# Fewer second keys in the first gate pass, and the fetched rows behind it, in a retention, convolution and expert-retrieval step

## The chip, the cores and the metric

The kernel runs on one core of a Trainium2 chip. The core has five engines that run side by side, each with its own queue taken in order: TensorE (PE; its weight loads are listed as PEld), VectorE (DVE), ScalarE (ACT), GpSimd (POOL) and SyncE (SP), which here only starts transfers. Sixteen DMA engines move data between the memory and the on-chip buffers. The metric is the device time of one execution in microseconds, lower is better.

## The reference

The step is one decoder layer for a prompt of 512 tokens and for 32 sampled tokens (8 sequences of 4): an input projection, retention and a convolution module side by side, an output projection and a layer norm. Behind these comes the part that the change touches, a retrieval of experts by product keys:

```python
q = (xb @ w_query).reshape(PEER_BLOCK, PEER_HEADS, PEER_DQ)     # 8 heads
s1 = jnp.einsum('phd,hkd->phk', q1, sub_keys_1)                  # 128 first keys
s2 = jnp.einsum('phd,hkd->phk', q2, sub_keys_2)                  # 128 second keys
v1, i1 = lax.top_k(s1, PEER_TOPK)                                # 16 of each
v2, i2 = lax.top_k(s2, PEER_TOPK)
...                                                              # the best 16 of the pairs
idx = e1 * N_KEYS + e2                                           # one of 16384 experts
gate = jax.nn.softmax(sv)
u = jnp.take(peer_u, idx, axis=0)
act = jax.nn.gelu(jnp.einsum('phkd,pd->phk', u, xb))
vv = jnp.take(peer_v, idx, axis=0)
out = jnp.einsum('phk,phkd->pd', gate * act, vv)
```

So each token takes 8 x 16 = 128 experts. Each is a row of 1024 numbers in the first table (u) and one in the second (v). The output is the gated sum of second-table rows, and a second layer norm ends the layer.

## The kernel before

The retrieval is done in two ways at once.

**Fetched rows.** For the first 288 tokens (two groups of 128 prompt tokens and the 32 sampled ones) the rows are fetched. One indirect transfer (L564, GpSimd's queue) brings the u and the v row of one expert for each of 128 partitions, 1 MB. VectorE takes the dot with the token (L567), ScalarE the gelu and the gate (L569, L570), and VectorE adds the weighted v row to a running sum (L575). The first group of 128 tokens has 128 such rows and is done ahead of the stages that matter here. Then come the sampled group "s" (32 tokens, spread over four times as many partitions, 32 rows) and the second prompt group "b" (128 rows), 160 rows in all. The transfers share three buffers (pool `gp`), and a buffer is free when its v row has been added.

**Whole tables.** For the last 256 prompt tokens (`ND`) both tables are read whole, one second key at a time: a key `e` covers 128 experts, so a tile of each table is 512 KB, and SyncE loads it into one of five buffers (pool `uvp`, `UV = 5`).

- `scores_of(e)` (L774) multiplies the u tile with the 256 tokens, and ScalarE applies the gelu.
- `build` makes the gates. For eight tokens at a time (`TB`) VectorE writes a one-hot table over the first keys (`A`, L847), one over the second keys (`M`, L849), and `B`, which is `M` times the gate in three bf16 parts (L852). TensorE multiplies `A` with `B`, three products a token (L858), so that a token's gates lie as 128 first keys by `ne` second keys in PSUM. The tables have two buffers each, and so has the PSUM tile.
- `v_stage(e)` (L893) multiplies key `e`'s gated scores, from a tile `GW`, with the v tile, and adds into four PSUM banks (`pB`), eight matmul records a key.

All 128 keys' gated scores for 256 tokens don't fit at once, so the keys lie in four tiles, `EG = (32, 20, 44, 32)` from `E0S = (0, 32, 52, 96)`: Gb, Gc, Ga and Gd. The scores of Ga and Gb (76 keys) are made first. `first_keys` builds the gates of keys 0 to 95 and multiplies them into Gb and Ga (L872); into Gc, whose scores don't exist yet, it copies them (L870). `last_keys` builds those of 96 to 127 once Gb's keys have been used and its room is free, and ScalarE copies them into Gd (L878). For Gc and Gd `s_stage(e)` makes the scores late and VectorE multiplies them in (L885).

`run((phases(), 1), (fetched(), 2))` interleaves the two ways in program order, one key's step to two rows. The program order isn't the order on the chip: a scheduler orders each engine's queue ahead of time, from its own estimate of when each instruction can start. `behind(a, b)` adds an order between two instructions for that scheduler. On the chip each engine then takes its queue strictly as written.

`finish` ends a fetched group: residual, layer norm, and an output transfer in SyncE's queue (L585), among the table loads. The last layer norm (L445 to L453) reads the four PSUM banks, and L945 stores its result.

Of the kernel before, what the change touches and what calls it, by code (L numbers as in the profile page):

```python
# [8 lines left out]
F32 = mybir.dt.float32  # L9
# [4 lines left out]
AF = mybir.ActivationFunctionType  # L14
OP = mybir.AluOpType
# [3 lines left out]
D = 1024  # L19
# [5 lines left out]
PH, NK, TK = 8, 128, 16  # L25
# [5 lines left out]
ND = NR - NG2  # L31
TB = 8
KX = 60
UV = 5
EG = (32, 20, 44, 32)
E0S = (0, 32, 52, 96)

ROWS = [(a, TK // (a + 1)) for a in range(TK)]
NCAND = sum(n for _, n in ROWS)
# [52 lines left out]
def tile_step(ctx: ExitStack, tc: tile.TileContext, a, o):  # L92
    nc = tc.nc
    V, S, T, G = nc.vector, nc.scalar, nc.tensor, nc.gpsimd
# [68 lines left out]
    def behind(ins, other):  # L163
        tc.add_manual_dep(ins.ins, other.ins.name, mybir.DependencyInfo(
            mybir.DependencyClass.NoSync, mybir.DependencyReason.DATA), reason="order")
# [342 lines left out]
    def retrieve(q_of, hs, w, r, E, gate, e0, later=None):  # L508
# [47 lines left out]
        V.reciprocal(sm[:n], sm[:n])  # L556
        V.tensor_mul(gate[:n, e0:e0 + nh], ex[:n], sm[:n].unsqueeze(2).to_broadcast([n, nh, TK]))

    def gather(x1, idx, gate, acc, slots):

        for k in slots:
            t = (gx.tile([128, 2 * D], F32, name="g") if x1 is x1_0 and k < KX and k % 4 == 3 else
                 gp.tile([128, 2 * D], F32, name="g"))
            G.indirect_dma_start(out=t, out_offset=None, in_=a["uv"],  # L564
                                 in_offset=bass.IndirectOffsetOnAxis(ap=idx[:, k:k + 1], axis=0))
            act = gw.tile([128, 2], F32, name="act")
            V.scalar_tensor_tensor(t[:, :D], t[:, :D], 1.0, x1, op0=OP.mult, op1=OP.mult, accum_out=act[:, 0:1])  # L567
            wgt = gw.tile([128, 1], F32, name="wgt")
            S.activation(act[:, 1:2], act[:, 0:1], AF.Gelu)  # L569
            S.activation(wgt, act[:, 1:2], AF.Copy, scale=gate[:, k:k + 1])  # L570
            v = t[:, D:]
            if k == slots[0]:
                S.activation(acc, v, AF.Copy, scale=wgt)
            else:
                V.scalar_tensor_tensor(acc, v, wgt, acc, op0=OP.mult, op1=OP.add)  # L575
            yield
# [72 lines left out]
    pm, last = mix_mm(128, g0, y0, 0, wo)  # L649
# [100 lines left out]
    gap = ctx.enter_context(tc.tile_pool(name="gap", bufs=1, reuse_waits="tile"))  # L750
# [7 lines left out]
    banks[:] = [pq]  # L758
    load_keys()
    ln2 = [bc_row("lng", a["ln2_g"], D), bc_row("lnb", a["ln2_b"], D)]  # L760
    GW = {2: gap.tile([128, EG[2], ND], F32, name="Ga")}

    def place(e):

# [30 lines left out]
    for g in range(2):  # L795
# [9 lines left out]
        p = mmps().rearrange("p (q t) -> p q t", q=4)  # L805
# [10 lines left out]
                V.tensor_sub(gr, gr, gtT[:, q, cs])  # L816
    topk_of("b", NS, range(0, PH, 2))
    topk_of("s", 0, range(2))
    for e in range(E0S[2], E0S[3]):
        S.activation(place(e), scores_of(e), AF.Gelu)  # L820
    gbs = ExitStack()
    gb = gbs.enter_context(tc.tile_pool(name="gb", bufs=1, side="right", reuse_waits="tile"))
    GW[0] = gb.tile([128, EG[0], ND], F32, name="Gb")
    for e in range(EG[0]):
        S.activation(place(e), scores_of(e), AF.Gelu)
# [7 lines left out]
    gc = ctx.enter_context(tc.tile_pool(name="gc", bufs=1, reuse_waits="tile"))  # L833
    pacc = ctx.enter_context(tc.tile_pool(name="pacc", bufs=1, space=PSUM, reuse_waits="tile"))
    pB = [[pacc.tile([128, 512], F32, name=f"pB{b}{q}") for q in range(2)] for b in range(2)]
    for b in range(2):
        for q in range(2):
            residual(pB[b][q], x1T, range(q * 4, q * 4 + 4), NG2 + b * 128)
    GW[1] = gc.tile([128, EG[1], ND], F32, name="Gc")

    def build(bt, e0, ne, nt):


        pt = None
        for t1 in range(0, ND, TB):
            A = bt.tile([128, NK, TB], BF, name="A")
            V.tensor_tensor(A, iot, e1T[:, t1:t1 + TB].unsqueeze(1).to_broadcast([128, NK, TB]), op=OP.is_equal)  # L847
            M = bt.tile([128, ne, TB], BF, name="M")
            V.tensor_tensor(M, iot[:, e0:e0 + ne],  # L849
                            e2T[:, t1:t1 + TB].unsqueeze(1).to_broadcast([128, ne, TB]), op=OP.is_equal)  # L850
            B = bt.tile([128, 3, ne, TB], BF, name="B")
            V.tensor_tensor(B, M.unsqueeze(1).to_broadcast([128, 3, ne, TB]),  # L852
                            gtT[:, :, t1:t1 + TB].unsqueeze(2).to_broadcast([128, 3, ne, TB]), op=OP.mult)
            for t in range(t1, t1 + TB):
                if t % nt == 0:
                    pt = pdn.tile([128, nt, ne], F32, name="mm")
                for q in range(3):
                    T.matmul(pt[:, t % nt], A[:, :, t - t1], B[:, q, :, t - t1], start=(q == 0), stop=(q == 2))  # L858
                if t % nt == nt - 1:
                    yield pt, slice(t - nt + 1, t + 1)  # L860

    def first_keys():

        with tc.tile_pool(name="bt", bufs=2, reuse_waits="tile") as bt:
            for pt, ts in build(bt, 0, E0S[3], 4):
                for g in range(3):
                    to = GW[g][:, :, ts]
                    part = pt[:, :, E0S[g]:E0S[g + 1]].rearrange("p t e -> p e t")
                    if g == 1:
                        V.tensor_copy(to, part)  # L870
                    else:
                        V.tensor_mul(to, to, part)  # L872

    def last_keys():

        with tc.tile_pool(name="bt", bufs=2, reuse_waits="tile") as bt:
            for pt, ts in build(bt, E0S[3], EG[3], 16):
                S.activation(GW[3][:, :, ts], pt.rearrange("p t e -> p e t"), AF.Copy)  # L878
                yield

    def s_stage(e):

        W = dw_.tile([128, ND], F32, name="W")
        S.activation(W, scores_of(e), AF.Gelu)
        V.tensor_mul(place(e), place(e), W)  # L885

    def v_stage(e):
        vt = uvp.tile([128, D], F32, name="uv")
        nc.sync.dma_start(vt, a["uv"][e * NK:(e + 1) * NK, D:])
        W = place(e)  # L890
        for b in range(2):
            for q in range(2):
                T.matmul(pB[b][q], W[:, b * 128:(b + 1) * 128], vt[:, q * 512:(q + 1) * 512],  # L893
                         start=False, stop=(e == NK - 1), skip_group_check=True)

    def phases():
        for e in range(EG[0]):
            v_stage(e)
            if e < EG[1]:
                s_stage(E0S[1] + e)  # L900
            yield
        gbs.close()
        gd = ctx.enter_context(tc.tile_pool(name="gd", bufs=1, side="right", reuse_waits="tile"))
        GW[3] = gd.tile([128, EG[3], ND], F32, name="Gd")
        b = last_keys()
        more = iter(range(E0S[3], NK))
        for e in range(E0S[1], E0S[3]):
            v_stage(e)
            if next(b, "end") == "end":
                for _ in range(1):  # L910
                    k = next(more, None)
                    if k is not None:
                        s_stage(k)
            yield
        for e in range(E0S[3], NK):
            v_stage(e)
            yield

    def fetched():
# [15 lines left out]
            finish(x1g, [ac[:, 0:512], ac[:, 512:]], w_, [(0, w_, dst)], t)  # L935
            yield

    first_keys()
    run((phases(), 1), (fetched(), 2))
    for b in range(2):  # L940
        t = uvp.tile([128, D], F32, name="uv")
# [50 lines left out]
```

## Time and profile before

| | us |
|---|---|
| median of 3 runs | 1728.95 |
| lowest and highest of them | 1721.68, 2358.62 |
| the profiled run | 1726.13 |
| its span in the trace | 1724.4 |
| TensorE busy | 1610.5 |
| VectorE busy | 1282.7 |
| ScalarE busy | 391.4 |
| GpSimd busy | 386.5 |

The profile is of one execution. It gives busy time by engine, by stretch of time and by group of equal instructions, says what ended the idle time ahead of an instruction ("<-"), and follows back the chain of work that ended last. PEclk is the TensorE clock that was granted, as a share of full speed; the DMA share is the mean busy share of the sixteen DMA engines. A group's row has the line, the engine, the operation, what it writes and reads, its shape and count, then its busy time and mean duration, and then the idle time of its engine ahead of it. Neighbouring instructions of an engine overlap a little at their ends, so start-to-start distances are a few hundredths shorter than durations.

### The profile page before, as it was taken

What the parts mean: (1) busy time and instruction counts of PE and PEld (TensorE: products, weight loads), DVE (VectorE), ACT (ScalarE), POOL (GpSimd) and SP (SyncE); (2) the same over time, 40 slices, a digit from 0 to 9 for tenths busy, and PEclk for the clock granted to TensorE, in tenths of its full rate; (3) what the DMA queues carried; (4) which work ended last, traced back from release to release, by engine and by line L of the source; (5) the groups of instructions that cost most, each with busy time, mean ns of one, the idle gap of its engine ahead of it and who ended that gap; (6) DMA issues with size and microseconds to landing.
All of it is one profiled execution on the core that took longest, in us unless ns stands there. A gap on an engine that the chain in (4) does not pass through costs nothing.

```text
span 1724.4 us, 20025 instructions
## 1 busy us (share of the span) xinstructions
PE 1610.5 (93%) x7014; PEld 1123.9 (65%) x7014; DVE 1282.7 (74%) x3044; ACT 391.4 (23%) x1091; POOL 386.5 (22%) x335
## 2 busy tenths in 40 slices
PE   7899999969599999999998888999999999999997
PEld 6887566547455678888886565665557776664443
DVE  4949998898759999999679899665466665556631
ACT  1324541452223233333210011111111111111100
POOL 1001321445312222201211113222122222232200
PEclk9899999989889999999985656999999999999999
DMA  9459778978987799955965436999877899999952
GB/s 364 156 204 377 256 266 291 346 273 291 355 310 284 260 368 351 350 191 211 367 228 183 171 98 226 405 354 362 335 294 283 292 368 364 367 358 398 421 209 98
DMA packets 99537, 503.71 MB, mean 292 GB/s; under 512 B 10183, under 2 KB 21191, under 8 KB 56549
## 3 DMA queue, kind: packets, MB, share of 16 engines
q0 software_dynamic: 42240, 305.12, 47.3%
q1 hardware_dynamic: 50749, 189.96, 29.8%
q10 hardware_dynamic: 6448, 7.36, 1.3%
q8 instruction: 55, 0.90, 0.2%
q14 instruction: 45, 0.37, 0.1%
HBM read 497.03 MB, written 5.80 MB: 292 GB/s over the span
## 4 chain that ended last, share of the span: by engine, by line
PE 55%; DVE 30%; DMA 8%; issue 3%; POOL 1%; ACT 1%; SPq 0%; DVEq 0%; ACTq 0%; POOLq 0%
PE pB L893 26%; PE sp L774 13%; PE mm L196 8%; DVE acc L575 6%; DVE g L567 5%; PE mm L858 5%; DMA g<-in_uv_dram,I 4%; DVE B L852 2%; DMA g<-in_w_in_dram 1%; DVE pick L549 1%; DVE oh L546 1%; DMA out_dram<-keys 1%; DMA keys<-in_state_retention_dram 1%; DVE score L503 1%; PE mm L306 1%
## 5 line engine op out<-in xcount | busy, mean ns | idle before, releaser
L774 PE MATMUL sp<-x1T,uv 128*128 128x256 f32 x2048 | 467.5, 384 | 11.3 <-ACT Ga L820 5.8
L774 PEld LDWEIGHTS sp<-x1T,uv 128*128 128x128 f32 x2048 | 390.0, 193 | 83.6 <-issue 15.7
L575 DVE SCALAR_TENSOR_TENSOR acc<-g,wgt,acc 128x1024 f32<-128x1024 f32 x285 | 364.8, 1280 | 79.5 <-ACT wgt L570 78.7
L564 POOL DMA_INDIRECT g<-in_uv_dram,Ib x128 | 155.9, 1218 | 502.4 <-DVE acc L575 404.9
L564 POOL DMA_INDIRECT g<-in_uv_dram,I x128 | 160.4, 1254 | 436.7 <-DVE acc L575 207.3
L567 DVE SCALAR_TENSOR_TENSOR g<-g,x1g 128x1024 f32<-128x1024 f32 x160 | 195.3, 1222 | 63.9 <-DMA g<-in_uv_dram,Ib 51.5
L858 PE MATMUL mm<-B,A 128*128 128x96 bf16 (+1 forms) x1536 | 195.6, 300 | 25.3 <-DVE Ga L872 25.3
L569 ACT ACTIVATE act<-act 128x1 f32<-128x1 f32 x288 | 58.0, 201 | 679.5 <-DVE g L567 679.4
L858 PEld LDWEIGHTS <-A 128*128 128x128 bf16 x1536 | 162.6, 151 | 69.9 <-DVE Ga L872 33.6
L196 PE MATMUL mm<-x1T,w 128*128 128x384 f32 (+1 forms) x512 | 181.1, 508 | 0.7 <-ACT on L426 0.7
L567 DVE SCALAR_TENSOR_TENSOR g<-g,x 128x1024 f32<-128x1024 f32 x128 | 155.6, 1216 | 26.4 <-DMA g<-in_uv_dram,I 24.3
L893 PE MATMUL pB<-uv,Ga 128*128 128x512 f32 x352 | 156.1, 593 | 0.0
L196 PEld LDWEIGHTS mm<-x1T,w 128*128 128x128 f32 x512 | 98.0, 194 | 73.8 <-issue 42.1
L893 PE MATMUL pB<-uv,Gb 128*128 128x512 f32 x256 | 118.0, 613 | 0.4 <-DVE Gb L872 0.4
L893 PEld LDWEIGHTS pB<-uv,Ga 128*128 128x128 f32 x352 | 66.8, 190 | 71.3 <-issue 69.8
L893 PE MATMUL pB<-uv,Gd 128*128 128x512 f32 x256 | 110.0, 592 | 0.0
L893 PEld LDWEIGHTS pB<-uv,Gd 128*128 128x128 f32 x256 | 48.6, 190 | 61.2 <-issue 60.7
L893 PEld LDWEIGHTS pB<-uv,Gb 128*128 128x128 f32 x256 | 50.2, 198 | 56.3 <-issue 54.6
L847 DVE TENSOR_TENSOR A<-iot,e1T 128x1024 bf16<-128x1024 bf16 x64 | 43.9, 687 | 49.3 <-PE mm L858 49.3
L564 POOL DMA_INDIRECT g<-in_uv_dram,Is x32 | 35.9, 1123 | 183.3 <-DVE acc L575 131.4
L893 PE MATMUL pB<-uv,Gc 128*128 128x512 f32 x160 | 72.7, 607 | 0.0
L196 PE MATMUL mm<-g,w 128*128 128x160 f32 (+1 forms) x512 | 69.7, 294 | 3.0 <-ACT score L522 2.6
(274 smaller groups left out, 1695.0 us busy)
## 6 DMA issues: line engine op xcount, KB each, us to landing
uv<-in_ut_dram SPq DMA_DIRECT2D x128, 512.0 KB
uv<-in_uv_dram SPq DMA_DIRECT2D x128, 512.0 KB
w<-in_w_in_dram SPq DMA_DIRECT2D x18, 1024.0 KB
w<-in_w_query_dram SPq DMA_DIRECT2D x16, 1024.0 KB
w<-in_w_out_dram SPq DMA_DIRECT2D x7, 1024.0 KB
g<-in_uv_dram,I POOLq DMA_INDIRECT x128, 7.7
keys<-in_state_retention_dram ACTq DMA_DIRECT2D x4, 512.0 KB
out_dram<-keys SPq DMA_DIRECT2D x4, 512.0 KB
```

Of the source, the lines that this page charges most:

```text
L196: T.matmul(p[:, :n], w[m // 2][:, k, (m % 2) * 128:(m % 2 + 1) * 128], xT[:, k, c0:c0 + n], start=(k == 0), stop=(k == 7))
L306: mm = T.matmul(p[:n, q * 256:(q + 1) * 256], xT[:, k, c0:c0 + n], w[q][:, k, :], start=(k == 0), stop=(k == 7))
L503: V.match_replace(s, dst[:, 0:8], s, -3.0e38)
L564: G.indirect_dma_start(out=t, out_offset=None, in_=a["uv"], in_offset=bass.IndirectOffsetOnAxis(ap=idx[:, k:k + 1], axis=0))
L567: V.scalar_tensor_tensor(t[:, :D], t[:, :D], 1.0, x1, op0=OP.mult, op1=OP.mult, accum_out=act[:, 0:1])
L569: S.activation(act[:, 1:2], act[:, 0:1], AF.Gelu)
L575: V.scalar_tensor_tensor(acc, v, wgt, acc, op0=OP.mult, op1=OP.add)
L774: T.matmul(sp, u[:, k], x1T[:, k, NG2:], start=(k == 0), stop=(k == 7))
L847: V.tensor_tensor(A, iot, e1T[:, t1:t1 + TB].unsqueeze(1).to_broadcast([128, NK, TB]), op=OP.is_equal)
L852: V.tensor_tensor(B, M.unsqueeze(1).to_broadcast([128, 3, ne, TB]), gtT[:, :, t1:t1 + TB].unsqueeze(2).to_broadcast([128, 3, ne, TB]), op= ...
L858: T.matmul(pt[:, t % nt], A[:, :, t - t1], B[:, q, :, t - t1], start=(q == 0), stop=(q == 2))
L893: T.matmul(pB[b][q], W[:, b * 128:(b + 1) * 128], vt[:, q * 512:(q + 1) * 512], start=False, stop=(e == NK - 1), skip_group_check=True)
```

## The change

`EG` becomes `(32, 44, 20, 32)` and `E0S` `(0, 32, 76, 96)`: the 44 keys of Ga now follow the 32 of Gb, so the first pass covers keys 0 to 75, whose scores all exist, and has no copies. The other 52 keys go through `last_keys`, eight tokens a PSUM tile where it was sixteen, with two ScalarE copies each, behind the first 32 keys' products. Their scores (52 `s_stage` calls) all come behind that, two for each later key step; 20 of them stood with the first 32 key steps. And each dot of a row that is fetched once the first pass is written gets an order behind the pass's last multiplication.

```diff
-EG = (32, 20, 44, 32)
-E0S = (0, 32, 52, 96)
+EG = (32, 44, 20, 32)
+E0S = (0, 32, 76, 96)
...
+    fence = []
+
     def gather(x1, idx, gate, acc, slots):
...
-            V.scalar_tensor_tensor(t[:, :D], t[:, :D], 1.0, x1, op0=OP.mult, op1=OP.mult, accum_out=act[:, 0:1])
+            dot = V.scalar_tensor_tensor(t[:, :D], t[:, :D], 1.0, x1, op0=OP.mult, op1=OP.mult, accum_out=act[:, 0:1])
+            if fence:
+                behind(dot, fence[0])
...
-    GW = {2: gap.tile([128, EG[2], ND], F32, name="Ga")}
+    GW = {1: gap.tile([128, EG[1], ND], F32, name="Ga")}
...
-    for e in range(E0S[2], E0S[3]):
+    for e in range(E0S[1], E0S[2]):
         S.activation(place(e), scores_of(e), AF.Gelu)
...
-    GW[1] = gc.tile([128, EG[1], ND], F32, name="Gc")
+    GW[2] = gc.tile([128, EG[2], ND], F32, name="Gc")
...
-            for pt, ts in build(bt, 0, E0S[3], 4):
-                for g in range(3):
+            for pt, ts in build(bt, 0, E0S[2], 4):
+                for g in range(2):
                     to = GW[g][:, :, ts]
-                    part = pt[:, :, E0S[g]:E0S[g + 1]].rearrange("p t e -> p e t")
-                    if g == 1:
-                        V.tensor_copy(to, part)
-                    else:
-                        V.tensor_mul(to, to, part)
+                    last = V.tensor_mul(to, to, pt[:, :, E0S[g]:E0S[g + 1]].rearrange("p t e -> p e t"))
+        return last
...
-            for pt, ts in build(bt, E0S[3], EG[3], 16):
-                S.activation(GW[3][:, :, ts], pt.rearrange("p t e -> p e t"), AF.Copy)
+            for pt, ts in build(bt, E0S[2], EG[2] + EG[3], 8):
+                for g in (2, 3):
+                    S.activation(GW[g][:, :, ts], pt[:, :, E0S[g] - E0S[2]:E0S[g] - E0S[2] + EG[g]].rearrange("p t e -> p e t"), AF.Copy)
                 yield
...
             v_stage(e)
-            if e < EG[1]:
-                s_stage(E0S[1] + e)
             yield
...
-        more = iter(range(E0S[3], NK))
-        for e in range(E0S[1], E0S[3]):
+        more = iter(range(E0S[2], NK))
+        for e in range(E0S[1], NK):
             v_stage(e)
             if next(b, "end") == "end":
-                for _ in range(1):
+                for _ in range(2):
                     k = next(more, None)
                     if k is not None:
                         s_stage(k)
-            yield
-        for e in range(E0S[3], NK):
-            v_stage(e)
             yield
...
-    first_keys()
+    fence.append(first_keys())
```

## The prediction

> **What bounds the kernel now.** I read the page first, then busy time by stretch, then the chain that ended last. The span is 1724.4 us and the profiled run 1726.13 us, 1.7 us around the span; the median shown is 1728.95 us, 0.2% above.
>
> ```profile
> span 1724.4 us, 20025 instructions
> PE 1610.5 (93%) x7014; PEld 1123.9 (65%) x7014; DVE 1282.7 (74%) x3044; ACT 391.4 (23%) x1091; POOL 386.5 (22%) x335
> ```
>
> ```profile
> core 0: us, PE busy (x) PEld busy (x) DVE busy (x) ACT busy (x) POOL busy (x), PEclk, DMA share, GB/s
> 870.00:1061.00 191.00, 165.70 (x828) 126.38 (x828) 173.56 (x360) 20.10 (x63) 34.76 (x29) 0.62 0.48 163
> 1187.00:1236.00 49.00, 49.00 (x126) 22.13 (x125) 26.62 (x32) 6.66 (x25) 12.52 (x11) 1.00 0.96 374
> 1380.00:1548.00 168.00, 168.00 (x597) 113.18 (x596) 94.58 (x129) 25.34 (x94) 44.89 (x35) 1.00 0.95 364
> 1548.00:1650.00 102.00, 102.00 (x239) 45.22 (x238) 64.34 (x77) 13.01 (x53) 22.28 (x23) 1.00 0.99 403
> ```
>
> ```profile
> 869.88 3.69 PE sp L774 x16
> 873.58 8.54 PE mm L858 x48
> ...
> 1061.59 11.79 PE pB L893 x20
> ...
> 1530.55 3.45 PE sp L774 x16
> ...
> 1547.77 164.81 PE pB L893 x384
> ```
>
> The stretches show two regimes. From 873.6 to 1061.6 us VectorE is busy 173.6 of 191 us while the DMA share is 0.48: that is the first pass (one-hot tables, gate products, multiplication into the scores) with fetched rows worked in between. From 1061.6 to 1712.6 us TensorE never stops: 3.45 us for one key's scores, 164.81/48 = 3.43 us for one key's second-table product. In that regime the fetched rows run beside TensorE, and the memory is full too (0.99 at 403 GB/s in the last such stretch).
>
> **The change, part by part.** (a) *The first pass loses its fetched rows.* The next rows are one group of eight tokens on VectorE, then row work and products in the pass, then TensorE's rhythm.
>
> ```profile
> 1008.92 0.27 DVE L872 TENSOR_TENSOR Gb<-Gb,mm 128x128 f32<-128x128 f32 x1
> 1009.12 0.22 DVE L870 COPY Gc<-mm 128x80 f32<-128x80 f32 x1
> 1009.27 0.32 DVE L872 TENSOR_TENSOR Ga<-Ga,mm 128x176 f32<-128x176 f32 x1
> 1009.51 0.27 DVE L872 TENSOR_TENSOR Gb<-Gb,mm 128x128 f32<-128x128 f32 x1
> ...
> 1010.11 0.67 DVE L847 TENSOR_TENSOR A<-iot,e1T 128x1024 bf16<-128x1024 bf16 x1
> 1010.71 1.34 DVE L852 TENSOR_TENSOR B<-M,gtT 128x2304 bf16<-128x2304 bf16 x1
> 1011.98 0.54 DVE L849 TENSOR_TENSOR M<-iot,e2T 128x768 bf16<-128x768 bf16 x1
> 1012.45 1.28 DVE L582 SCALAR_TENSOR_TENSOR yt<-x1g,acc 32x512 f32<-32x512 f32 x2
> ```
>
> ```profile
> L567 DVE SCALAR_TENSOR_TENSOR g<-g,x1g 128x1024 f32<-128x1024 f32 x29 | 35.1, 1215 | 2.6 <-DMA g<-in_uv_dram,Is 2.6
> L575 DVE SCALAR_TENSOR_TENSOR acc<-g,wgt,acc 128x1024 f32<-128x1024 f32 x27 | 34.5, 1278 | 1.9 <-ACT wgt L570 1.8
> L893 PE MATMUL pB<-uv,Gb 128*128 128x512 f32 x20 | 10.9, 689 | 0.0
> ```
>
> ```profile
> 1004.98 4.47 PE L858 MATMUL mm<-B,A 128*128 128x96 bf16 x24 [0.21 <-DVE Ga L872]
> ```
>
> ```profile
> 1248.27 3.05 PE L858 MATMUL mm<-B,A 128*128 128x32 bf16 x48
> 1251.15 10.52 PE L893 MATMUL pB<-uv,Gc 128*128 128x512 f32 x20
> ```
>
> Start to start a group costs VectorE 1.19 (six evacuations) + 0.60 + 1.27 + 0.47 = 3.53 us, plus some 2.5 us where a row lies in it. The change takes away both copies (0.15 each) and shrinks M and B to 76/96: 0.90 + 0.60 + 1.01 + 0.37 = 2.88 us. TensorE's 24 products of 96 columns took 4.47 us, 0.186 each; 48 of 32 columns took 2.88 us (1248.27 to 1251.15), 0.060 each. The price follows the columns, so I take 0.186 x 76/96 = 0.147 us for 76, which 0.060 x 76/32 = 0.143 bears out. The ends are 0.186 (no gain from fewer columns) and 0.120, under which it no longer matters, since 24 of those are VectorE's 2.88 us. 24 x 0.147 = 3.54 us is more than 2.88: **TensorE becomes the bound of the pass**. Buffers allow that: two tables and two PSUM tiles are held, and VectorE finishes the next tables 2.4 us into the 3.5 us of the group before.
>
> [...] The granted clock was 0.62 over the pass. [...]
>
> The pass would start one score sooner, since the built order of the changed kernel has 76 scores ahead where 77 lay: 873.6 - 3.5 = 870.1. It has 31 groups left: 31 x 3.54 = 109.7, and the same 20 early product halves, 10.9. **End of the pass: 990.7 us, 71 us sooner.**
>
> (b) *TensorE's work behind it.* By the built order there follow, up to the last score's multiplication on VectorE, 87.5 second-table products, all 52 late scores (four ran inside or ahead of the pass before) and the second build of 52 columns: 300.1 + 179.4 + 768 x 0.0975 (0.060 x 52/32) = 74.9, and 3.2 for the slow start seen in the 20 at 1061.59 (11.79 against 8.6). That sums to 557.6: the last late score at 1548.3. Ends for the 52 columns: 0.060 (28.8 less) and 0.101 (2.7 more). Behind it 38 products, 130.3: TensorE ends at **1678.6**, against 1712.6.
>
> (c) *ScalarE's two copies a group.*
>
> ```profile
> L878 ACT ACTIVATE Gd<-mm x16: 592/597/599, 1228.1 to 1375.6; 128x512 f32<-128x512 f32 x16
> ```
>
> 64 smaller copies at no more than 0.6 us are 38 us beside 9.6 now, on an engine busy 23%, each hidden under the 3.43 us of table product that TensorE has between two groups: I cost them at nothing. Without that cover one would cost 0.3 to 0.6 us a group, under 20 us.
>
> (d) *The fetched rows, where I expect the loss.* In the order of before, 40 of the 160 rows' dots stand in or ahead of the pass; in the new order none. VectorE takes its queue in order, and a late score's multiplication or a table waits there for TensorE with the next rows' dots, and so the release of their three buffers, behind it. The new order puts 25 dots ahead of the second build's fifth table, 52 ahead of the first late score's multiplication, 103 ahead of the last: **57 rows remain when the last score is done, against 25 before.** Their price:
>
> ```profile
> 819.78 1.22 DVE L567 SCALAR_TENSOR_TENSOR g<-g,x1g 128x1024 f32<-128x1024 f32 x1
> ...
> 821.60 1.29 DVE L575 SCALAR_TENSOR_TENSOR acc<-g,wgt,acc 128x1024 f32<-128x1024 f32 x1 [0.60 <-ACT wgt L570]
> 822.80 1.22 DVE L567 SCALAR_TENSOR_TENSOR g<-g,x1g 128x1024 f32<-128x1024 f32 x1
> ```
>
> ```profile
> L567 DVE SCALAR_TENSOR_TENSOR g<-g,x1g x24: 1224/1225/1227, 1553.6 to 1647.1; 128x1024 f32<-128x1024 f32 x24
> ```
>
> ```profile
> DMA to landing us min/median/max: 8.2/8.4/10.6
> ```
>
> ```profile
> DMA to landing us min/median/max: 5.4/5.7/7.4
> ```
>
> ```profile
> 1685.14 10.63 SPq L889 DMA_DIRECT2D uv<-in_uv_dram  x4
> ```
>
> With rows ready, dot to dot is 3.02 us, the floor. Beside products and their loads it was (1647.1 - 1553.6)/23 = 4.07 us: landing took 8.4 us (stretch 1540 to 1660). Where SyncE loaded no table (940 to 1000) it took 5.7; with the 3.1 from a dot's start to its sum's end (819.78 to 822.89) that is 8.8 us for one of three buffers, 2.9 a row, under the floor. That was with fewer rows in flight, so I take 3.2 between 3.02 and 4.07, nearer to the floor. Table loads ended 16.8 us ahead of TensorE, so here at 1661.8: 113.5/4.07 = 28 rows by then, the other 29 x 3.2 = 92.8. **Last row: 1754.6.**
>
> [...]
>
> (e) *The end.* In the new order the last layer norms of both the fetched group and the products stand behind the last row on VectorE.
>
> ```profile
> 1656.74 1.23 DVE L453 TENSOR_TENSOR yt<-yt,lnb 128x1024 f32<-128x1024 f32 x1
> ...
> 1710.04 0.70 DVE L445 BATCH_NORM_STATS2 lst<-pB 128x6 f32<-128x512 f32 x1 [52.07 <-PE pB L893]
> ...
> 1717.95 1.28 DVE L453 TENSOR_TENSOR uv<-uv,lnb 128x512 f32<-128x512 f32 x2
> ```
>
> The first took from 1650.3 to 1658.0, 7.7 us, the second 1710.0 to 1719.2, 9.2, and 5.2 to the span's end; overlapping a little, 20 in all.
>
> (f) *SyncE.* The small group's output waits in its queue and everything behind it too:
>
> ```profile
> SPq L585 <- DVE yt L453: 136.3, 1, 136.3
> ```
>
> It stood behind five product loads; now it stands behind 53, with the loads of the 54th and on queued behind it, five tiles ahead of TensorE. A late norm would stop TensorE: 0 to 10 us, I take 3.
>
> Sum: 1754.6 + 20 + 3 = 1777.6, and 1.7 around the span: **1779 us, 3.1% above 1726.13.**
>
> **The rivals.**
> *TensorE still ends it* (faster). Then 1678.6 + 11.8 + 1.7 = 1692 us, or 1663 with the cheap 52 columns. For it: TensorE is the bound today and the pass gives back 71 us. Against: it decides at 130.3/57 = 2.3 us a row, and the floor is 3.02. Chance 0.05.
> *52 columns cost what 32 do*, if the weight load sets the price: 1779 - 28.8 = 1750. Against: 96 columns cost three times 32. 0.15.
> *The clock is released in the pass*, so VectorE binds it: 31 x 2.88 = 89.3, 20 less, 1759. For it: the pass would have no gaps. 0.1. [...]
> *76 columns cost what 96 do*: 31 x 24 x 0.039 = 29 more, 1808. 0.1.
> *Rows stay at 4.07 after the table loads end*, because their own queue limits them: 29 x 0.87 = 25 more, 1804. 0.1.
> That the dots don't go behind the pass is excluded by the built order.
>
> **How the numbers follow.** The forecast has 0.5, with 1757 to 1800 of its own. A measurement of this kernel can tell about 2%, 1692 to 1761 around the profiled run. Slower: the forecast but for its lowest part, and the two upper rivals, 0.67; within: 1750, 1759 and that part, 0.29; faster 0.04. The range leaves out TensorE's case, and the corners where several ends meet: 1742 to 1812.
>
> **What would show it.** Right: the pass ends near 991 with TensorE busy throughout and no row in it; TensorE's last product near 1679; VectorE's rows going on 70 to 80 us past it at near 3.2 us; the chain ending in rows and their fetches. Wrong: TensorE's product last in the chain, rows under 2.5 us, a build product of 52 columns at 0.06, or TensorE waiting for a table load near the 54th product.

## The result, and the profile after

The changed kernel takes 1800.09 us (median of six runs, 1796.43 to 1803.89) against 1728.76 before (median of six too). One run of before stood far above the others (2358.62), and the ratio leaves it out. The ratio is **1.042, with a 95% interval of 1.0394 to 1.0446**: slower, as forecast. The profiled run took 1796.46 us; the forecast was 1779, in a range of 1742 to 1812.

Lines below are those of the changed kernel: the scores are L778, the build products L862, the second-table products L895, a fetched row's dot L569 and its sum L579. First the page: the span, busy time by engine, and the chain that ended last, by engine and by line.

```profile
span 1794.5 us, 20069 instructions
PE 1615.0 (90%) x7014; PEld 1152.9 (64%) x7014; DVE 1277.8 (71%) x2980; ACT 399.9 (22%) x1139; POOL 388.5 (22%) x335
...
PE 50%; DVE 24%; DMA 16%; issue 7%; POOL 2%; ACT 2%; DVEq 0%; SPq 0%; POOLq 0%; ACTq 0%
```

TensorE does the same work as before (1615 us busy, 1610.5 before), in a span 70 us longer. Its timeline shows when, with start and duration first:

```profile
864.02 53.29 PE L862 MATMUL mm<-B,A 128*128 128x76 bf16 x372 [1.04 <-DVE Ga L872]
...
933.55 49.82 PE L862 MATMUL mm<-B,A 128*128 128x76 bf16 x348
983.74 6.79 PE L895 MATMUL pB<-uv,Gb 128*128 128x512 f32 x11 [0.38 <-DVE Gb L872]
...
1551.17 7.07 PE L778 MATMUL sp<-x1T,uv 128*128 128x256 f32 x32
1558.08 20.76 PE L895 MATMUL pB<-uv,Gc 128*128 128x512 f32 x48
1578.68 110.03 PE L895 MATMUL pB<-uv,Gd 128*128 128x512 f32 x256
```

The pass now runs as two solid blocks of products and ends at 983.74 instead of 1061.59. TensorE ends at 1688.71, 24 us sooner than before. Not all of these 78 us are the change's: the profiled run of before was already 8 us later when the tables' first score began (503.8 against 496.0), ahead of the stages that the change touches. So the pass gained some 70 us. Behind it TensorE needs 705 us where it needed 651. Of these 54 us, the four late scores that used to be inside or ahead of the pass are 14, the 52 columns in the second build where 32 were are 30, and the rest comes with a lower clock (below). The rest of the loss lies behind TensorE's end, in the fetched rows. These are their dots from the last late score to the end of the table loads, their transfers, and the same two views behind that:

```profile
L569 DVE SCALAR_TENSOR_TENSOR g<-g,x1g x29: 1215/1224/1227, 1560.3 to 1671.5; 128x1024 f32<-128x1024 f32 x29
DMA to landing us min/median/max: 8.0/8.4/9.4
```

```profile
L569 DVE SCALAR_TENSOR_TENSOR g<-g,x1g x28: 1216/1224/1226, 1675.5 to 1773.1; 128x1024 f32<-128x1024 f32 x28
DMA to landing us min/median/max: 5.6/6.6/8.1
```

29 + 28 = 57 rows, the number that the built order leaves. They come at (1671.5 - 1560.3)/28 = 3.97 us each beside the table loads and (1773.1 - 1675.5)/27 = 3.61 us behind them. The last part of the chain, in order of time (start, duration, what; the longer pieces), is made of them and of the short steps between:

```profile
1750.18 6.55 DMA g<-in_uv_dram,Ib
1756.79 1.11 issue
1758.59 1.29 DVE acc L579
1760.33 3.14 issue
1763.69 6.31 DMA g<-in_uv_dram,Ib
...
1774.88 1.30 DVE acc L579
1776.20 1.29 DVE yt L586 x2
```

A row lands, is used, a buffer comes free, the next row is fetched. The "issue" from 1760.33 on is GpSimd waiting for that buffer, as the timeline shows:

```profile
1762.14 1.28 DVE L579 SCALAR_TENSOR_TENSOR acc<-g,wgt,acc 128x1024 f32<-128x1024 f32 x1 [0.60 <-ACT wgt L574]
1763.69 1.68 POOL L566 DMA_INDIRECT g<-in_uv_dram,Ib  x1 [2.61 <-DVE acc L579]
```

The sum ends at 1763.42, and the next fetch starts 0.27 us later. The stretches show the two regimes, and two things the sum did not have:

```profile
core 0: us, PE busy (x) PEld busy (x) DVE busy (x) ACT busy (x) POOL busy (x), PEclk, DMA share, GB/s
910.00:950.00 40.00, 40.00 (x212) 32.34 (x210) 23.49 (x56) 0.00 (x0) 0.00 (x0) 0.67 0.00 1
1200.00:1250.00 50.00, 50.00 (x213) 29.54 (x213) 28.52 (x42) 7.42 (x28) 11.15 (x8) 0.84 0.70 256
1250.00:1300.00 50.00, 50.00 (x224) 33.64 (x223) 26.13 (x39) 7.45 (x29) 10.51 (x7) 0.79 0.58 210
1600.00:1650.00 50.00, 50.00 (x118) 22.13 (x117) 31.92 (x40) 6.47 (x26) 12.17 (x13) 1.00 1.02 421
1700.00:1750.00 50.00, 0.00 (x0) 0.00 (x0) 34.08 (x42) 6.97 (x28) 17.86 (x13) 0.50 0.81 298
```

In the pass the DMA engines stand idle (0.00): the memory time that the rows used there before is lost, and it is wanted later. Between 1200 and 1300 us the granted clock falls to 0.84 and 0.79 although TensorE is busy throughout. From 1700 on TensorE has nothing left while VectorE is busy 34 of 50 us and the memory 0.81.

### The profile page after: what moved, and what is told of

It reads as the page before. It is cut to its first block, busy times and chain, and to the rows that moved or that the text cites. A ratio compares the mean times of both kernels' runs of the same rounds, so it can differ in the third digit from the quotient of the medians.

```text
span 1794.5 us, 20069 instructions
## 1 busy us (share of the span) xinstructions
PE 1615.0 (90%) x7014; PEld 1152.9 (64%) x7014; DVE 1277.8 (71%) x2980; ACT 399.9 (22%) x1139; POOL 388.5 (22%) x335
## 4 chain that ended last, share of the span: by engine, by line
PE 50%; DVE 24%; DMA 16%; issue 7%; POOL 2%; ACT 2%; DVEq 0%; SPq 0%; POOLq 0%; ACTq 0%
PE pB L895 18%; PE sp L778 12%; PE mm L862 10%; DMA g<-in_uv_dram,Ib 8%; PE mm L196 7%; DVE acc L579 6%; DMA g<-in_uv_dram,I 5%; DVE g L569 4%; DMA g<-in_w_in_dram 1%; DVE pick L549 1%; POOL g L566 1%; DVE oh L546 1%; DMA out_dram<-keys 1%; DVE score L503 1%; DVE iu L502 1%
## 5 line engine op out<-in xcount | busy, mean ns | idle before, releaser
L778 PE MATMUL sp<-x1T,uv 128*128 128x256 f32 x2048 | 462.9, 385 | 10.2 <-ACT Ga L824 6.1
L778 PEld LDWEIGHTS sp<-x1T,uv 128*128 128x128 f32 x2048 | 392.3, 193 | 80.1 <-issue 12.5
L579 DVE SCALAR_TENSOR_TENSOR acc<-g,wgt,acc 128x1024 f32<-128x1024 f32 x285 | 364.4, 1279 | 95.0 <-ACT wgt L574 94.2
L566 POOL DMA_INDIRECT g<-in_uv_dram,Ib x128 | 161.7, 1264 | 456.6 <-DVE acc L579 419.5
L569 DVE SCALAR_TENSOR_TENSOR g<-g,x1g 128x1024 f32<-128x1024 f32 x160 | 195.1, 1221 | 64.2 <-DMA g<-in_uv_dram,Ib 46.8
L862 PEld LDWEIGHTS <-A 128*128 128x128 bf16 x1536 | 188.6, 146 | 18.6 <-issue 13.4
L862 PE MATMUL mm<-B,A 128*128 128x76 bf16 (+1 forms) x1536 | 192.9, 302 | 1.0 <-DVE Ga L872 1.0
L569 DVE SCALAR_TENSOR_TENSOR g<-g,x 128x1024 f32<-128x1024 f32 x128 | 155.1, 1212 | 24.8 <-DMA g<-in_uv_dram,I 24.0
L895 PE MATMUL pB<-uv,Ga 128*128 128x512 f32 x352 | 169.2, 631 | 0.0
L895 PEld LDWEIGHTS pB<-uv,Ga 128*128 128x128 f32 x352 | 69.9, 204 | 75.9 <-issue 75.3
L895 PE MATMUL pB<-uv,Gb 128*128 128x512 f32 x256 | 118.1, 620 | 0.4 <-DVE Gb L872 0.4
L895 PE MATMUL pB<-uv,Gd 128*128 128x512 f32 x256 | 110.0, 592 | 0.0
L895 PEld LDWEIGHTS pB<-uv,Gb 128*128 128x128 f32 x256 | 50.4, 200 | 61.0 <-issue 60.3
L895 PEld LDWEIGHTS pB<-uv,Gd 128*128 128x128 f32 x256 | 48.7, 190 | 61.2 <-issue 59.8
L895 PE MATMUL pB<-uv,Gc 128*128 128x512 f32 x160 | 71.1, 592 | 0.0
```

Of the source, the lines that this page charges most:

```text
L566: G.indirect_dma_start(out=t, out_offset=None, in_=a["uv"], in_offset=bass.IndirectOffsetOnAxis(ap=idx[:, k:k + 1], axis=0))
L569: dot = V.scalar_tensor_tensor(t[:, :D], t[:, :D], 1.0, x1, op0=OP.mult, op1=OP.mult, accum_out=act[:, 0:1])
L778: T.matmul(sp, u[:, k], x1T[:, k, NG2:], start=(k == 0), stop=(k == 7))
```

## The experiments

The theory: the end is the later of two streams, TensorE's and the fetched rows', and the change moved the second one, because VectorE's order leaves 57 rows behind the last late multiplication. Rivals: TensorE's longer work behind the pass, the memory, the price of the build products. The kernel before ran beside each set and took 1722.32, 1726.6 and 1721.53 us; ratios are to it.

**The new split without the wait.**

```diff
-    fence.append(first_keys())
+    first_keys()
```

> The changed kernel without the wait: 76 keys in the first pass and 52 in the second, but the fetched rows' dots stand among the pass again. In the built order 17 rows are left when the last late multiplication comes (57 in the changed kernel, 25 in the kernel before). Theory (the end is set by the rows that the built order leaves to the tail, and TensorE's own path became longer by the split): 40 rows go into the pass, about 5.3 us a group, so the pass ends near 1040 instead of 984; TensorE's work behind it is the changed kernel's, 574 + 131 us, so TensorE ends near 1745, 17 rows at 4 us are through long before, and with the 12 us end and 1.7 us about 1757 (1735 to 1775): slower than before by 1 to 2.5%, with TensorE last in the chain. Rival A (the wait alone made the loss, the split costs nothing): as before, 1728. Rival B (the split alone made the loss): about 1800.

Measured: 1732.05 us, ratio 1.0047 (1.002 to 1.0073). TensorE was last, as expected, but 25 us sooner than I worked out, so the number is a miss. TensorE's timeline; its waits in the pass, with the total, the count and the longest; and two stretches, in the columns above:

```profile
1030.12 10.85 PE L895 MATMUL pB<-uv,Gb 128*128 128x512 f32 x20 [1.07 <-DVE Gb L872]
...
1610.33 110.03 PE L895 MATMUL pB<-uv,Gd 128*128 128x512 f32 x256
```

```profile
PE mm L862 <- DVE Ga L872: 38.5, 27, 3.4
```

```profile
1200.00:1250.00 50.00, 50.00 (x278) 33.45 (x277) 32.23 (x49) 7.92 (x32) 13.64 (x8) 1.00 0.73 251
1250.00:1300.00 50.00, 50.00 (x271) 33.00 (x269) 33.68 (x50) 8.73 (x34) 9.96 (x7) 1.00 0.72 251
```

The rows cost the pass 38.5 us of TensorE's waiting and it ended at 1030, 10 us sooner than I took. Behind it TensorE needed 690 us where it needed 705 in the changed kernel, for the same products. The difference stands in the last fence: the granted clock stayed at 1.00. In this kernel's order the second build goes 24 products, one key's table products, 24; in the changed kernel's seven of the last eight bursts are of 48. That became a theory of its own, tested below. So the split alone costs 0.5%, and hardly the 4.2.

**The wait without the new split.**

```diff
+            dot = V.scalar_tensor_tensor(t[:, :D], t[:, :D], 1.0, x1, op0=OP.mult, op1=OP.mult, accum_out=act[:, 0:1])
+            if fence:
+                behind(dot, fence[0])
...
-    first_keys()
+    fence.append(first_keys())
```

> The kernel before with the wait alone: 96 keys in the first pass, 32 in the second, no late scores moved, but every later row's dot behind the pass's last multiplication. In the built order 65 rows are left at the last late multiplication (25 in the kernel before), and 80 of the 128 second-table products stand ahead of it. Theory (rows in the tail set the end): the pass ends near 1018 instead of 1061 (31 groups at 24 x 0.18 us and 11 us of halves), the last late score near 1518, TensorE ends near 1685, but 65 rows follow: 41 at 4.0 us beside the table loads to 1683, 24 at 3.6 us to 1770, with the 18 us end about 1788 (1770 to 1805), slower than before by 2 to 4.5% although TensorE is done over 40 us sooner. Rival A (TensorE's work sets the end): 1698. Rival B (the wait costs nothing, the split did): 1728 or less.

Measured: 1783.89 us, ratio 1.0348 (1.0277 to 1.0419), as expected to 4 us. TensorE's last products, and the dots from 1500 us on:

```profile
1567.98 110.03 PE L898 MATMUL pB<-uv,Gd 128*128 128x512 f32 x256
```

```profile
L569 DVE SCALAR_TENSOR_TENSOR g<-g,x1g x68: 1217/1225/1243, 1501.5 to 1760.8; 128x1024 f32<-128x1024 f32 x68
```

TensorE ended at 1678, 34 us sooner than before, and the rows went on to 1761, at 259.3/67 = 3.87 us each. The loss is nearly the whole of the changed kernel's, and the two parts add up: 0.5 + 3.5 = 4.0%, against 4.2.

**The last 57 rows left out**, so that part of the output lacks their terms.

```diff
-            yield from gather(x1g, Ig[g], GTg[g].rearrange("p h k -> p (h k)"), ac, range(128 // r_))
+            yield from gather(x1g, Ig[g], GTg[g].rearrange("p h k -> p (h k)"), ac, range(32 if r_ > 1 else 71))
```

> The changed kernel with the last 57 fetched rows of the third group of tokens left out, so that part of its output lacks their terms; nothing else is changed. Theory: TensorE's stream is untouched and ends where it did in the changed kernel, near 1689; no row stands behind it, and with an end of 12 us and 1.7 us the time is about 1703 (1690 to 1712). What is above that in the changed kernel, 97 us, is then the price of the 57 rows in the tail. Rival A (the rows also slow the table loads and through them TensorE's last products): TensorE ends 10 us or more sooner, 1690 or less. Rival B (the tail is set by TensorE's products or the table loads): no more than 20 us gained, 1780.

Measured: 1701.47 us in one run. TensorE's last block:

```profile
1579.10 110.03 PE L895 MATMUL pB<-uv,Gd 128*128 128x512 f32 x256
```

It starts within half a microsecond of where it does in the changed kernel. So the rows in the tail took nothing from TensorE, and what they cost is 1796.46 - 1701.47 = **95 us**, all of it behind TensorE. The run only prices the tail: it does less work than the kernel before, so the two can't be set against each other.

**The same rows, placed sooner.** VectorE's order was changed so that 28 rows are left instead of 57; `after_row(ins, n)` puts an instruction behind the n-th row's dot.

```diff
+            if e0:
+                late[0] += 1
+                if late[0] > 4:
+                    after_row(ins, 18 + 1.5 * late[0])
...
-        V.tensor_mul(place(e), place(e), W)
+        late[1] += 1
+        after_row(V.tensor_mul(place(e), place(e), W), 66 + 1.25 * late[1])
```

> The changed kernel with the same work, in another order on VectorE: the second build's masks from the fifth on stand behind row 18 + 1.5 n, the k-th late multiplication behind row 66 + 1.25 k, so that 28 rows instead of 57 are left at the last late multiplication (which stands behind 92 second-table products). Theory (the end is set by the rows that the built order leaves to the tail): 129 rows between 984 and the last late score need 4.4 us each, which the pace of 3.6 to 4.0 us seen in the tail allows; TensorE ends near 1690 and the 28 rows, 112 us at 4.0 us, a little before it; with the 12 us end about 1705 (1692 to 1730), 5% below the changed kernel and 1.4% below the kernel before. Rival A (rows come at 5 us or more while TensorE streams, so that VectorE's order holds the late multiplications up and TensorE waits): TensorE ends 40 to 80 us later, 1740 to 1780. Rival B (the number of rows left doesn't set the end): 1800.

Measured: 1762.25 us, ratio 1.0201 (1.0144 to 1.0258). Rival A held. What TensorE waited for behind the pass:

```profile
PE mm L871 <- DVE A L856: 18.0, 6, 5.3
PE pB L905 <- DMA uv<-in_uv_dram: 13.7, 9, 2.5
PE sp L783 <- ACT W L895: 3.4, 4, 1.8
```

The rows did not come at 4.4 us while TensorE streamed (130 dots from 985.0 to 1621.5, 4.93 us each), so the masks stood behind them in VectorE's queue, TensorE stood behind the masks, and its last product ended at 1737. It is 38 us better than the changed kernel all the same. The number left in the tail matters, but order alone lowers it at the price of TensorE's waiting: the rows must also be able to come sooner.

**Bursts of 24.** The one thing added is an order of the second build's products against the table products (`lastv` holds the last one of them).

```diff
+                    if e0 and t % nt == 0 and q == 0:
+                        behind(mm, lastv[0])
```

> The changed kernel with one thing more: the first of every 24 products of the second build stands behind the four products of a second-table block, so that TensorE's order is 24 build products, 4 table products, 24, 4, all through the second build; in the changed kernel the last seven bursts are of 48. 57 rows are left at the last late multiplication, as in the changed kernel. Theory (bursts of 48 of the small build products lower the granted clock for the large ones behind them): the granted clock is 1.00 through the second build (0.84 and 0.79 between 1200 and 1300 in the changed kernel), TensorE ends near 1673 instead of 1689; the rows behind the last late score start up to 15 us sooner, so the time is 1785 (1778 to 1802). Rival (the clock falls by the share of build products in a stretch, in whatever bursts): the same dip, TensorE ends at 1685 to 1692, 1800.

Measured: 1783.89 us, ratio 1.0333 (1.0304 to 1.0363), as expected to 1 us. The same two stretches, and on TensorE the end of the pass and the last block:

```profile
1200.00:1250.00 50.00, 50.00 (x275) 33.29 (x273) 33.06 (x49) 8.40 (x34) 13.45 (x9) 1.00 0.78 267
1250.00:1300.00 50.00, 50.00 (x241) 34.66 (x240) 30.11 (x42) 8.96 (x34) 12.47 (x9) 1.00 0.84 298
```

```profile
986.69 3.78 PE L897 MATMUL pB<-uv,Gb 128*128 128x512 f32 x4 [0.38 <-DVE Gb L874]
...
1566.69 110.03 PE L897 MATMUL pB<-uv,Gd 128*128 128x512 f32 x256
```

The clock stays at 1.00 and the last block starts 12.0 us sooner (1566.69 against 1578.68), although this run's pass ended 3 us later (986.69 against 983.74). With the same products between, that stretch is 14.9 us shorter. So the dip comes with the long bursts, and it is a fifth of the change's loss.

**The build's columns side by side, first form.** Both builds store `B` so that TensorE reads the columns of a token next to each other; VectorE writes it with large steps.

```diff
-            B = bt.tile([128, 3, ne, TB], BF, name="B")
-            V.tensor_tensor(B, M.unsqueeze(1).to_broadcast([128, 3, ne, TB]),
+            B = bt.tile([128, 3, TB, ne], BF, name="B")
+            V.tensor_tensor(B.rearrange("p q t e -> p q e t"), M.unsqueeze(1).to_broadcast([128, 3, ne, TB]),
...
-                    T.matmul(pt[:, t % nt], A[:, :, t - t1], B[:, q, :, t - t1], start=(q == 0), stop=(q == 2))
+                    T.matmul(pt[:, t % nt], A[:, :, t - t1], B[:, q, t - t1], start=(q == 0), stop=(q == 2))
```

> The changed kernel with the mask product B stored token by token, so that the operand that TensorE streams has its 76 or 52 columns side by side and not 16 bytes apart; VectorE writes it with that stride instead. 57 rows are left at the last late multiplication. Theory A (a build product costs 1.9 ns a column because of the 16 byte steps): products of 76 columns fall from 0.143 us to about 0.07, the pass is then bound by VectorE at 2.9 us a group or more and ends near 970 instead of 984, and the second build's 768 products at 0.05 instead of 0.10 save some 38 us: TensorE ends near 1640, the time is about 1750. Theory B (the columns themselves or the weights cost it): 0.143 and 0.100 us stay, TensorE ends near 1689, the time is 1800. In both, if VectorE's B becomes dearer than 1.10 us by over 0.8 us, VectorE bounds the pass instead and it ends later than 984.

Measured: 2016.34 us, ratio 1.1694 (1.1661 to 1.1726). A step of the first pass on TensorE, and VectorE's `B`:

```profile
880.67 1.74 PE L862 MATMUL mm<-B,A 128*128 128x76 bf16 x24 [7.75 <-DVE Ga L872]
```

```profile
L856 DVE TENSOR_TENSOR B<-M,gtT 128x1824 bf16<-128x1824 bf16 x29 | 226.5, 7812 | 0.0
```

Both readings came out. A product fell from 0.143 to 1.74/24 = 0.073 us, which is theory A: half of its price was the 16-byte step. And `B` rose from 1.10 to 7.81 us on VectorE, which then bounds the pass and more. Why a step of 16 bytes costs that much was not shown.

**A fourth buffer for the rows**, paid with the fifth of the tables.

```diff
-UV = 5
+UV = 4
...
+                 gl[0].tile([128, 2 * D], F32, name="g") if gl and x1 is not x1_0 and k % 4 == 3 else
...
+    gl.append(ctx.enter_context(tc.tile_pool(name="gl", bufs=1, reuse_waits="tile")))
```

> The changed kernel with a fourth buffer for fetched rows (every fourth row of the last two groups of tokens lies in it) from the pass on, and four instead of five for the tables. The built order then puts more rows ahead of the late multiplications: 22 are left at the last one, not 57. Theory (a row's own trip through its buffer, landing, dot, gate and addition, sets the pace with three buffers: the run with 28 left held 4.9 us a row while TensorE streamed, the tail 3.6): with four buffers the pace is 3.7 us or less, TensorE hardly waits and ends at 1690 to 1700, and the 22 rows end ahead of it: about 1707 (1695 to 1730). Rival A (transfers share one limit, so that a fourth buffer only lengthens each landing): rows stay near 4.9 us while TensorE streams, VectorE's order holds the late multiplications up, TensorE ends near 1770, 1785. Rival B (four table buffers are too few): TensorE waits for tables between 984 and 1690, in rows of the trace that name the tables' transfers, 1720 to 1760.

Measured: 1732.91 us, ratio 1.0048 (1.0007 to 1.0089). The dots (durations, first and last start) and a stretch while TensorE streams, first of this kernel, then of the changed one:

```profile
L570 DVE SCALAR_TENSOR_TENSOR g<-g,x1g x95: 1217/1225/1267, 1299.3 to 1649.2; 128x1024 f32<-128x1024 f32 x95
```

```profile
1300.00:1650.00 350.00, 346.24 (x1177) 216.51 (x1176) 253.98 (x335) 66.25 (x240) 96.03 (x95) 1.00 1.02 423
```

```profile
L569 DVE SCALAR_TENSOR_TENSOR g<-g,x1g x30: 1215/1219/1226, 1403.9 to 1550.0; 128x1024 f32<-128x1024 f32 x30
```

```profile
1400.00:1550.00 150.00, 150.00 (x581) 110.12 (x580) 84.57 (x119) 23.80 (x90) 40.17 (x29) 1.00 0.96 359
```

A row takes 349.9/94 = 3.72 us with four buffers and 146.1/29 = 5.04 with three. So with a fourth buffer, and the order built around it, the rows come sooner, as the theory has it, and the change's loss is all but gone. The buffers are not the whole of the difference: with three of them and VectorE's order changed (the same rows, placed sooner) 75 dots came from 1305.4 to 1621.5, 4.27 us each, so part of the 5.04 is the order. Then the next limit shows: a DMA share of 1.02 at 423 GB/s for 350 us on end. The tables come a little late, two scores and a table product take 11.1 us instead of 10.3, and TensorE ends at 1721.8, not at 1700. The time lies in rival B's range. The full DMA share speaks for the memory, rival A's limit at a later point than I had it; whether a fifth table buffer would have helped is not shown, as it was taken away in the same run.

**The kernel before, with the wait from the 25th row on.**

```diff
+                count[0] += 1
+                if count[0] > 24:
+                    behind(dot, fence[0])
```

> The kernel before with the wait for the rows from the 25th on alone: 24 rows keep their places in the pass, the others stand behind it. 42 rows are left at the last late multiplication (25 in the kernel before, 65 with the whole wait), where 48 of the 128 second-table products are left, 165 us. Theory (the end is the later of TensorE's stream and the rows that the order leaves to the tail): the pass ends near 1046 instead of 1062, TensorE ends near 1697 instead of 1713, and 42 rows at 4.0 us are through at about the same time, 1700; with an end of 12 to 18 us about 1713 (1705 to 1725), 0.3 to 1% below the kernel before. Rival A (any wait on the rows loses in proportion, 62 us for 40 rows): 1728 + 16 x 1.5 = 1750. Rival B (the pass isn't shortened by taking 16 rows out): 1724 to 1730.

Measured: 1716.98 us, ratio 0.9951 (0.993 to 0.9972). TensorE's last block and the dots from 1510 us on:

```profile
1580.12 110.03 PE L900 MATMUL pB<-uv,Gd 128*128 128x512 f32 x256
```

```profile
L569 DVE SCALAR_TENSOR_TENSOR g<-g,x1g x44: 1217/1225/1227, 1513.6 to 1691.5; 128x1024 f32<-128x1024 f32 x44
```

TensorE ends at 1690.2 and the last row starts at 1691.5: both streams end together. The same wait that costs 3.5% on all rows gains 0.5% on some of them.

**The second build's columns side by side, second form.** VectorE goes through the columns innermost, in the order in which they lie; the first pass is left alone.

```diff
+            if e0:
+                dims = [128, 3, TB, ne]
+                M = bt.tile([128, TB, ne], BF, name="M")
+                V.tensor_tensor(M, row[:, e0:e0 + ne].unsqueeze(1).to_broadcast([128, TB, ne]),
+                                e2T[:, t1:t1 + TB].unsqueeze(2).to_broadcast([128, TB, ne]), op=OP.is_equal)
+                B = bt.tile(dims, BF, name="B")
+                V.tensor_tensor(B, M.unsqueeze(1).to_broadcast(dims),
+                                gtT[:, :, t1:t1 + TB].unsqueeze(3).to_broadcast(dims), op=OP.mult)
...
-                    T.matmul(pt[:, t % nt], A[:, :, t - t1], B[:, q, :, t - t1], start=(q == 0), stop=(q == 2))
+                    T.matmul(pt[:, t % nt], A[:, :, t - t1], B[:, q, t - t1] if e0 else B[:, q, :, t - t1], start=(q == 0), stop=(q == 2))
```

> The changed kernel with the second build's mask product stored with its 52 columns side by side, as in the run with both builds so, but written in that order too: VectorE goes through the columns innermost, with the mask made in the same order and the gate value repeated along it. The first pass is left as it was. 57 rows are left at the last late multiplication. Theory (16 byte steps cost TensorE half of a build product's time; VectorE's 7.8 us for such a product came from writing it against its order): products of 52 columns fall from 0.100 to about 0.05 us, 38 us of TensorE's stream, and its bursts are too short to lower the clock, so the last late score ends near 1510 to 1520; the product on VectorE costs up to twice its 0.8 us, 32 x 0.8 = 26 us beside TensorE's stream; 57 rows follow, 33 at 4.0 and 24 at 3.6 us, to 1735, and 18 us: about 1757 (1740 to 1778). Rival A (VectorE's product stays near 6 us in this order too): VectorE holds the second build up by 32 x 5 = 160 us, 1850 and more. Rival B (the rows ahead of the last late multiplication, 100 at 5.7 us, already hold it up): 1785 to 1800.

Measured: 1750.53 us, ratio 1.0178 (1.0151 to 1.0206), 2.7% below the changed kernel's 1800.09. `B` on VectorE, one token group and its neighbour on TensorE, and TensorE's last block:

```profile
L858 DVE TENSOR_TENSOR B<-M,gtT 128x1248 bf16<-128x1248 bf16 x28 | 40.6, 1451 | 0.0
```

```profile
1098.68 1.59 PE L871 MATMUL mm<-B,A 128*128 128x52 bf16 x24
1100.11 3.68 PE L904 MATMUL pB<-uv,Ga 128*128 128x512 f32 x8
...
1527.69 110.03 PE L904 MATMUL pB<-uv,Gd 128*128 128x512 f32 x256
```

24 products take 1.43 us from start to start, 0.060 each instead of 0.100, `B` costs 1.45 instead of 0.80, and TensorE ends 51 us sooner, 7 of which it had already at the end of the pass (976.58 against 983.74). The rows still end it, at 1724 for the last dot.

**Both in the kernel before: 24 or 30 rows kept in the pass, and the second build so.**

```diff
-                if count[0] > 24:
+                if count[0] > 30:
```

> The kernel before with the wait for the rows from the 25th on alone (42 rows left at the last late multiplication, 48 second-table products left there) and the second build's 32 columns side by side, written in that order. Theory: 768 products fall from 0.060 to about 0.033 us, 21 us less in TensorE's stream, which ended at 1690 without this; 42 rows at 4.0 us after a last late multiplication near 1504 end near 1672 too: about 1690 (1680 to 1710), 2% below the kernel before. Rival A (rows and tables together already take the DMA engines' whole share from 1350 on, so the time saved is waited for again): 1707 to 1717, as without it. Rival B (VectorE's product dearer by 5 us): 1800 and more.

> As the run with 24 rows in the pass, with 30: 37 rows left at the last late multiplication instead of 42. Theory: six rows more in the pass lengthen it by 6 to 9 us, TensorE ends that much later, near 1677, and the rows 12 us before it: about 1695 (1684 to 1712), 5 us above the run with 24. Rival (the rows left in the tail still set the end with 24): 5 to 15 us below the run with 24.

Measured: 1707.48 us with 24, ratio 0.992 (0.9893 to 0.9948), and 1709.03 with 30, 0.992 (0.9898 to 0.9943). These are the best two, 0.8% below the kernel before and 5% below the changed one; between them nothing can be told. The gain is smaller than worked out, and the intervals overlap with that of the wait alone (0.993 to 0.9972), so nothing shows that the layout of `B` helped here. A burst of the second build of the run with 24:

```profile
1231.29 3.02 PE L873 MATMUL mm<-B,A 128*128 128x32 bf16 x48
1234.16 10.55 PE L909 MATMUL pB<-uv,Gc 128*128 128x512 f32 x24
```

48 products of 32 columns take 2.87 us, 0.060 each, exactly what they cost with the steps. And 52 columns side by side cost 0.060 too. So 0.060 is the least that any run here shows for such a product with its weight load, and my 0.033 was wrong: at 32 columns, laying them side by side saves nothing.

## Why the prediction was right, point by point

**The sign, the mechanism and the range were right.** The number, 1777.6 us of span, was 16.9 short of 1794.5. By its own steps:

(a) *The pass loses its rows and TensorE bounds it*: right. It started at 864.0 instead of 870.1, a product of 76 columns cost 53.29/372 = 0.143 us against 0.147, and it ended 7 us sooner than forecast. The 6 us at the start are luck: in the run with bursts of 24, whose pass is the same, the block began at 870.3, and the first score of all had been 6 us later too (501.9 against 496.0). From its start the block took 119.7 us, 120.6 forecast. The rival that VectorE binds it fell, and with it the ground given for it, that the clock rises in a pass without gaps: TensorE was busy for 40 us without one (910 to 950), and the granted clock there was 0.67. The full clock would not have made VectorE the bound either: products of 52 columns cost 0.0997 us, 1.92 ns a column, at a granted clock of 1.00 (1100 to 1150), as against 1.89 ns here.

(b) *TensorE's work behind it* was the first mis-sized term: 574.3 us to the last late score instead of 557.6. The run with bursts of 24 takes 559.4 for the same work (986.69 to 1546.09), so 14.9 of these 16.7 us come with the long bursts and their lower clock, which the sum did not have; 768 x (0.0997 - 0.0975) = 2 are the product's price. That 52 columns cost as 32 was rejected, and so was that 76 cost as 96. The 38 products behind it took 130.6 against 130.3.

(c) *ScalarE's copies for nothing*: TensorE was busy without a break from 984 to 1688, so they held up nothing that counts.

(d) *The rows* were the second mis-sized term: 218.1 us from the last late score to the end of the last sum, 206.3 forecast. The count of 57 was right, the pace beside the loads 3.97 against 4.07, but the pace behind them 3.61 against 3.2. The step that failed is a buffer's trip: I took 5.7 for the landing and 3.1 for the use, 8.8. Three buffers at 3.61 make 10.8. On average over the 28 rows of the changed kernel's tail the landing took 6.9 (median 6.6), the use 3.4 (3.1 in most rows, more where another row's work stands ahead of its sum), and 0.6 more pass between landing and dot and between release and fetch. So the landing, with three rows in flight, is the larger part of what was mis-sized.

(e) *The end*: 18.3 us (1776.2 to 1794.5) against 20. (f) *SyncE*: nothing against 3. The small group's output did hold its queue up, for 3.6 us, and TensorE waited for no table behind the pass.

The errors add up: -7 and +17 ahead of the last late score, +12 in the rows, -2 and -3 behind: +17. Without the 6 us of luck at the start they would add up to some 23. *TensorE still ends it* fell with the dots 84 us past TensorE's end. That rows stay at 4.07 behind the loads was too dear by about as much as 3.2 was too cheap.

What the prediction did not see is why the rows can't come sooner. It treated the 57 as a given of the order. The run with four buffers shows that the order and the buffers go together: in the changed kernel, with three, a row takes 5 us while TensorE streams and the built order leaves 57; with four, 3.7 us and 22. Another order with three buffers recovers 38 us, and TensorE waits for it. So with three a row moved out of the pass goes to the tail or holds TensorE up.

## What to carry to other kernels

Work taken out of one stage must find room in another: count what the built order leaves behind the last step of the engine that bounds the rest, and compare it with what that engine's last stretch can hide (here 130 us, some 33 rows). A wait that clears a stage is worth as many instructions as that stretch hides, and no more; in the kernel before, 24 rows left in the pass made a gain of a loss. Before an engine's time is saved, look whether its operand lies in steps: in the changed kernel, with 52 columns, the layout was worth 2.7%; with the 32 columns of the kernel before, a product's price did not move.

## What the runs showed of the hardware beyond that

A bf16 product of 128 weights against 32, 52 or 76 columns took 0.060, 0.100 and 0.143 us where the columns lay 16 bytes apart, and 0.060 (32 and 52) and 0.07 (76) side by side. On VectorE the same mask product took 1.10 us in the order of its memory and 7.81 against it, for 1824 bf16 elements.

Where the changed kernel has bursts of 48 such products with 52 columns in steps (4.8 us each), the granted clock was 0.84 and 0.79 (1200 to 1300); in the run with bursts of 24 (2.4 us) it was 1.00 there. With bursts of 48 side by side (2.9 us) it was 1.00 in the run with the second form and 0.97 in the run with 24 rows in the pass (1200 to 1300). Whether the length of the burst or the reading in steps does it can't be told from these runs.

The sixteen DMA engines held 423 GB/s for 350 us in the run with four buffers, at a share of 1.02. At this rate, by estimate, the 160 rows of 1.05 MB and 172 table tiles of 0.52 MB that follow the pass need some 610 of the 705 us that TensorE streams there.
